# A transformer block on one core: queries times cosines read from the projection's bank, S5's output from inputs ahead of that from states, and operands of the last norms copied to PSUM

## The chip, the core and the metric

The kernel runs on one core of a Trainium2 chip. The metric is the device time of one execution in microseconds (us), the median of the runs. Five engines run side by side, each through its own queue of instructions in a fixed order: TensorE (PE, with its weight loads PEld), VectorE (DVE), ScalarE (ACT), GpSimd (POOL) and SyncE (SP), which here only issues DMA transfers. An instruction that waits holds up all that stand behind it on its engine.

## What is computed

The reference is one block on a sequence of 1024 tokens of width 1024, all in float32, cut here to its skeleton:

```python
proj = x @ w_in + b_in
q, k, v, u, xr, gate = split(proj)            # 512, 128, 128, 256, 256, 256 columns
q, k = apply_rope(q), apply_rope(k)           # t*cos + swapped(t)*sin, per head of 64
y_attn = sliding_window_attention(q, k, v, sinks)
y_s5   = s5_mixer(u, ...)                     # complex diagonal scan, then y = C h + D u, gelu, gated
y_lru  = rg_lru_mixer(xr, gate, ...)          # convolution, gates, real scan
mix = group_rmsnorm((y_attn, y_s5, y_lru), g)
x = layer_norm(ALPHA * x + mix @ w_out + b_out, ln1_g, ln1_b)
f = (silu(conv(x @ w_gate)) * (x @ w_up)) @ w_down        # inner width 2816
x = layer_norm(ALPHA * x + f, ln2_g, ln2_b)
```

## The kernel before

Most float32 products are made as three products of a high and a low part (`mm3`, lines 144 to 146); ACT writes the high part and DVE subtracts it to get the low one (`split`, lines 119 and 120). So each weight (`whi`, `wlo`) passes through ACT and then DVE before PE can use it. All large SBUF tiles come from one pool of 47 slots of 128x1024 floats, all PSUM tiles from one pool of eight banks of 128x512 floats.

The work stands in three stages. `mixers` makes the projections of x tile by tile (`project`, each tile of 128 columns in two halves of 512 tokens, a half being 24 products into a bank `pin`, which ACT copies out with the bias, line 527), and beside them S5, the RG-LRU and the attention, whose steps are Python generators that a table (AGENDA) starts after given projections. A scheduler then puts the instructions of each engine in an order by its own estimate of times, so that the order on each queue is that of the order listings below and not quite that of the source.

- Rotation of a query tile (`turn`): SP copies the halves of each head, swapped, to `rsw` (line 639). DVE multiplies the tile by the cosines, both operands in SBUF (line 645, 128x1024), POOL multiplies `rsw` by the sines (646), DVE adds (647), then ACT and DVE split the sum in `qh` and `ql`, and three DMAs stack those (670 to 672). There are four query tiles.
- S5's output: for each of two halves h, eight products of inputs U with `Tz` (line 443) alternate with eight of states H with `CA` (444) in two banks; each pair fills one 128-column piece of a bank. ACT applies gelu (446), SP writes Y to DRAM in eight pieces (449) and reads it back in another layout (452), loads the gate's weight (457), and PE makes the gate product (469). The states come from DVE and POOL (lines 228 to 233), are moved by SP (431), and U has been there long before.
- `ffn` makes gate and up products and at its end the down product by a seven-product scheme (D_ORDER = 1, 2, 6, 7, 5, 4, 3, each of 11 items, 77 in all). Each item loads two tiles (`d_load`), splits them (`d_parts`) and makes 12 products in four banks (`d_product`). `d_load(i + 9)` and `d_parts(i + 5 + ...)` say how many items ahead of product i the loads and the splits are issued. The last `LAST` items are made bank by bank, so that the four token blocks 0 to 3 end one after another; the last bank is made in two halves of 256 columns.
- The last norm: blocks 4 to 7 end with product 4 and are normed during product 3, blocks 0 to 2 after their banks end (`norm`), block 3 last of all (lines 1520 to 1525). `norm` takes mean and variance, ACT scales each half of 512 columns (1462), then DVE does the first half and POOL the second half, each a product with `ln2_g` (1463) and a sum with `ln2_b` (1464) on SBUF operands, and SP writes the block out.

Of the kernel before, what the change touches and what calls it, by code (L numbers as in the profile page):

```python
# [13 lines left out]
AF = mybir.ActivationFunctionType  # L14
ALU = mybir.AluOpType
MULT, ADD, SUB, MAX, MIN = ALU.mult, ALU.add, ALU.subtract, ALU.max, ALU.min
# [30 lines left out]
L = 1024  # L47
# [9 lines left out]
NC5 = L // T5  # L57
# [20 lines left out]
class Trunk:  # L78
# [163 lines left out]
    def s5(self, ud):  # L242

        nc, I = self.nc, self.I
        v, po, S = nc.vector, nc.gpsimd, self.small
# [15 lines left out]
        x = S([128, NP], "s5x")  # L261
# [83 lines left out]
        Tz = []  # L345
# [88 lines left out]
        dy = self.dr.tile([NG, CH, T5, NC5], F32, name="dy")  # L434
        yg = []
        for h in range(2):
            Y = self.big([128, 8, NC5], f"s5Y{h}")
            pY = [self.ps([128, 4, NC5], f"s5pY{q}") for q in range(2)]
            for i in range(4):
                pr = h * 4 + i  # L440
                for q in range(2):
                    o = pY[q][:, i, :]
                    nc.tensor.matmul(o, Tz[q][:, pr, :], U[h][:, 2 * i + q, :], start=True, stop=False)
                    nc.tensor.matmul(o, CA[q][:, pr, :], H[h][:, q, i, :], start=False, stop=True)
            for q in range(2):
                nc.scalar.activation(Y.rearrange("p (r q) c -> p q r c", q=2)[:, q], pY[q], AF.Gelu_apprx_tanh)
            yield
            for i in range(T5):
                nc.sync.dma_start(out=dy[h * 8:h * 8 + 8, :, i, :].rearrange("g c t -> c g t"),
                                  in_=Y[i * CH:(i + 1) * CH])  # L450
            y = self.big([128, T5, NC5], f"s5y{h}")
            nc.sync.dma_start(out=y.rearrange("p j t -> p (j t)"),
                              in_=dy[h * 8:h * 8 + 8].rearrange("g c j t -> (g c) (j t)"))
            yg.append(y)
# [70 lines left out]
    def in_half(self, W, f, hf, t, func=AF.Identity):  # L525
        p = self.proj_half(W, self.X, hf, "pin")
        self.nc.scalar.activation(t[:, hf * 512:(hf + 1) * 512], p, func, bias=self.col("b_in", f))


# [111 lines left out]

    def rope1(self, t, sw):

        nc = self.nc
        nc.vector.tensor_tensor(out=t, in0=t, in1=self.cos, op=MULT)
        nc.gpsimd.tensor_tensor(out=sw, in0=sw, in1=self.sin, op=MULT)
        nc.vector.tensor_tensor(out=t, in0=t, in1=sw, op=ADD)

# [25 lines left out]

    def turn(self, t, nm):

        sw = self.rope0(t)
        yield
        self.rope1(t, sw)
        hl = self.halves(t, nm)  # L680
        yield
        (self.stack_k if nm == "k" else self.stack_q)(hl)
        yield
# [409 lines left out]
    D_ORDER = (1, 2, 6, 7, 5, 4, 3)  # L1093
    LAST = 6

# [134 lines left out]
    def mixers(self):  # L1230
# [89 lines left out]
        def project(j):  # L1320
# [8 lines left out]
            t = at[nm, i]  # L1329
            self.in_half(Ws[nm, i], fs[nm] + i, hf, t, AF.Gelu_apprx_tanh if nm == "gg" else AF.Identity)  # L1330
            if hf:
                del Ws[nm, i]
                done[nm, i] = at.pop((nm, i))
                if nm in ("xr", "gg"):
                    (xr if nm == "xr" else self.gg).append(done.pop((nm, i)))
# [4 lines left out]
        def turn(nm, i):  # L1340
            yield from self.turn(done.pop((nm, i)), nm)

# [77 lines left out]
    def ffn(self, out):  # L1420
# [27 lines left out]
        ps = {}  # L1448
        g2 = b2 = None
        stats = lambda tb, i, s: v.bn_stats(bn[tb][:, i], self.z[tb][:, s])  # L1450
        hs = slice(0, 512), slice(512, D)

        def norm(tb):
# [5 lines left out]
            o = self.big([128, D], "o")  # L1459
            for h, e in enumerate((v, nc.gpsimd)):  # L1460
                s = hs[h]
                nc.scalar.activation(z[:, s], z[:, s], AF.Identity, scale=r, bias=m)  # L1462
                e.tensor_tensor(out=z[:, s], in0=z[:, s], in1=g2[:, s], op=MULT)  # L1463
                e.tensor_tensor(out=o[:, s], in0=z[:, s], in1=b2[:, s], op=ADD)
                if tb == 2:
                    nc.sync.dma_start(out=out[0, tb * 128:(tb + 1) * 128, s], in_=o[:, s])
# [4 lines left out]
        for i in range(cut):  # L1471
# [4 lines left out]
            b = ps[{2: "X", 7: "Q", 4: "Q"}.get(p, "T")]  # L1476
            self.d_load(i + 9)
            self.d_parts(i + 5 + (max(0, i - cut + 12) // 3))
            self.d_product(i, b, range(4), f == 0, f == NP_ - 1)
# [8 lines left out]
            if f == NP_ - 1:  # L1488
                for c in range(4):
                    self.d_out(p, c, b)  # L1490
                    if p in (2, 5, 4):
# [6 lines left out]
                        else:  # L1498
                            stats(tb, p == 5, hs[p == 5])
            if p == 3 and 0 < f < 5:  # L1500
                with self.after(self.mm.ins):
                    norm(3 + f)
        T = ps["T"]
# [14 lines left out]
        mv, a, r = st[tb]  # L1518
        for s in hs:
            v.scalar_tensor_tensor(z[:, s], z[:, s], mv[:, 0:1], g2[:, s], SUB, MULT)  # L1520
        self.newton(r, a)
        o = self.big([128, D], "o")
        for s in hs:
            v.scalar_tensor_tensor(o[:, s], z[:, s], r, b2[:, s], MULT, ADD)
            nc.sync.dma_start(out=out[0, tb * 128:(tb + 1) * 128, s], in_=o[:, s])
# [75 lines left out]
```

## Time and profile before

| | us |
|---|---|
| median of 3 runs | 1019.26 |
| lowest and highest of them | 1018.61, 1205.99 |
| the profiled execution, its own time | 1018.53 |
| its span, first to last instruction | 1016.5 |
| PE busy in it | 965.5 |
| DVE, POOL, ACT busy | 769.8, 563.2, 490.2 |

The span is that of one execution, and its own time is 2.0 us longer for what lies around it. A PE that is busy is counted with modelled ends of its matmuls, so a busy share of 95% is not a claim that PE is at its best; what is lost to waits and to a lower granted clock is read from the rows of single stretches.

### The profile page before, as it was taken

How to read it: one execution, taken by the hardware profiler on the slowest of the kernel's cores; microseconds unless marked ns; L12 is line 12 of the kernel's file. 1: busy time of each engine (PE TensorE's matmuls, PEld its weight loads, DVE VectorE, ACT ScalarE, POOL GpSimd, SP SyncE). 2: the span in 40 equal slices, each digit the busy share in tenths (PEclk: the TensorE clock that was granted, in tenths of full speed). 3: DMA queues.
4: the chain of work that ended last, by engine and by line, in shares of the span. 5: the costliest groups of instructions: out<-in, count | busy, mean ns of one | idle time of the engine just before them, and what ended most of it. 6: DMA issues, size and time to landing. Idle time of an engine off the chain costs nothing.

```text
span 1016.5 us, 13355 instructions
## 1 busy us (share of the span) xinstructions
PE 965.5 (95%) x4512; PEld 792.9 (78%) x4512; DVE 769.8 (76%) x1262; ACT 490.2 (48%) x952; POOL 563.2 (55%) x409
## 2 busy tenths in 40 slices
PE   8998888999999998999999999999999999999993
PEld 6877757789888776778878778888887788888883
DVE  6899668798989787667776777665676699965388
ACT  5322366676744766435524534545547265444131
POOL 0465234669843784777886878653551799000053
PEclk9999899999999999999999999999999999999997
DMA  8422665443221201546556546312415798686213
GB/s 301 145 54 82 150 164 144 116 115 110 77 105 63 82 22 42 191 182 228 197 204 240 197 176 233 151 68 88 155 73 186 284 391 287 211 289 202 64 42 124
DMA packets 64740, 158.53 MB, mean 156 GB/s; under 512 B 9440, under 2 KB 14080, under 8 KB 64672
## 3 DMA queue, kind: packets, MB, share of 16 engines
q1 hardware_dynamic: 64672, 157.68, 45.3%
q8 instruction: 35, 0.57, 0.2%
q14 instruction: 33, 0.27, 0.1%
HBM read 104.90 MB, written 42.21 MB: 145 GB/s over the span
## 4 chain that ended last, share of the span: by engine, by line
PE 55%; DVE 17%; POOL 9%; DMA 8%; issue 6%; ACT 4%; SPq 1%; DVEq 0%; POOLq 0%; ACTq 0%
PE pg L144 7%; PE pg L146 7%; PE pg L145 7%; PE pdT L145 3%; DMA d<-in_ffn_w_down_dram 3%; PE pdT L146 3%; PE pdT L144 3%; PE po L144 2%; PE po L146 2%; PE po L145 2%; PE pdQ L145 2%; PE pdQ L146 2%; POOL dt L1128 2%; PE pdQ L144 2%; POOL d L1128 2%
## 5 line engine op out<-in xcount | busy, mean ns | idle before, releaser
L120 DVE TENSOR_TENSOR dpl<-draw,dph 128x1024 fp32r<-128x1024 f32 x77 | 121.3, 1614 | 30.1 <-ACT dph L119 28.3
L144 PE MATMUL pg<-xt,apart 128*128 128x512 f32 x352 | 137.3, 391 | 4.1 <-ACT foa L1006 1.4
L146 PE MATMUL pg<-xt,apart 128*128 128x512 f32 x352 | 136.3, 391 | 2.5 <-DVE apart L120 2.4
L145 PE MATMUL pg<-xt,apart 128*128 128x512 f32 x352 | 137.3, 390 | 1.1 <-DVE xt L932 1.1
L119 ACT ACTIVATE dph<-draw 128x1024 fp32r<-128x1024 f32 x77 | 80.0, 1058 | 86.4 <-DVE dpl L120 24.5
L120 DVE TENSOR_TENSOR apart<-s,apart 128x512 fp32r<-128x512 f32 x88 | 94.7, 1086 | 25.4 <-ACT apart L119 25.3
L144 PE MATMUL pg<-xb,apart 128*128 128x512 f32 x264 | 103.2, 391 | 1.4 <-ACT fob L1006 1.4
L145 PE MATMUL pg<-xb,apart 128*128 128x512 f32 x264 | 102.8, 389 | 0.0
L146 PE MATMUL pg<-xb,apart 128*128 128x512 f32 x264 | 102.7, 389 | 0.0
L119 ACT ACTIVATE apart<-s 128x512 fp32r<-128x512 f32 x88 | 53.9, 626 | 63.8 <-POOL s L941 62.4
L144 PEld LDWEIGHTS pg<-xt,apart 128*128 128x128 f32 x352 | 66.1, 188 | 20.3 <-ACT foa L1006 3.6
L146 PEld LDWEIGHTS pg<-xt,apart 128*128 128x128 f32 x352 | 66.1, 188 | 18.8 <-DVE apart L120 5.3
L1463 POOL TENSOR_TENSOR z<-z,ln_g 128x512 f32<-128x512 f32 x7 | 11.5, 1643 | 123.3 <-ACT z L1462 123.3
L145 PEld LDWEIGHTS pg<-xt,apart 128*128 128x128 f32 x352 | 66.1, 188 | 15.4 <-DVE xt L932 1.9
L120 DVE TENSOR_TENSOR apart<-raw,apart 128x512 fp32r<-128x512 f32 x66 | 72.9, 1106 | 5.4 <-ACT apart L119 5.4
L145 PE MATMUL pdT<-dpl,dph 128*128 128x512 f32 (+1 forms) x182 | 69.6, 383 | 1.7 <-DVE dpl L120 1.7
L146 PE MATMUL pdT<-dph,dpl 128*128 128x512 f32 (+1 forms) x182 | 69.4, 382 | 0.0
L144 PE MATMUL pdT<-dph 128*128 128x512 f32 (+1 forms) x182 | 66.5, 383 | 0.6 <-DVE z L1205 0.5
L144 PEld LDWEIGHTS pg<-xb,apart 128*128 128x128 f32 x264 | 49.6, 188 | 12.6 <-ACT fob L1006 2.2
L1062 POOL TENSOR_TENSOR fc<-fc,fob 128x512 f32<-128x512 f32 x11 | 18.7, 1702 | 71.2 <-DVE fob L1005 62.8
L1086 DVE SCALAR_TENSOR_TENSOR fc<-pg,pack,fc 128x511 f32<-128x511 f32 (+1 forms) x64 | 46.4, 742 | 15.1 <-ACT tail L1083 10.9
L146 PEld LDWEIGHTS pg<-xb,apart 128*128 128x128 f32 x264 | 49.6, 188 | 10.3
(483 smaller groups left out, 2628.9 us busy)
## 6 DMA issues: line engine op xcount, KB each, us to landing
draw<-h SPq DMA_DIRECT2D x77, 256.0 KB, 5.3
raw<-in_ffn_w_gate_dram SPq DMA_DIRECT2D x22, 512.0 KB, 5.0
raw<-in_ffn_w_up_dram SPq DMA_DIRECT2D x22, 512.0 KB, 4.1
h<-fc SPq DMA_DIRECT2D x22, 512.0 KB, 2.6
d<-in_ffn_w_down_dram SPq DMA_DIRECT2D x22, 512.0 KB, 6.7
draw<-d SPq DMA_DIRECT2D x44, 256.0 KB, 5.4
draw<-in_ffn_w_down_dram SPq DMA_DIRECT2D x33, 256.0 KB, 5.4
h<-hs SPq DMA_DIRECT2D x11, 512.0 KB, 3.6
```

The source lines that it names most:

```text
L119: self.hi = nc.scalar.activation(hi, src, AF.Copy)
L120: e.tensor_tensor(out=lo, in0=src, in1=hi.bitcast(F32), op=SUB)
L144: self.mm = nc.tensor.matmul(out, ah, bh, start=first, stop=False, skip_group_check=more)
L145: nc.tensor.matmul(out, ah, bl, start=False, stop=False, skip_group_check=more)
L146: nc.tensor.matmul(out, al, bh, start=False, stop=last, skip_group_check=more)
L1062: e.tensor_tensor(out=c[:, one], in0=c[:, one], in1=x, op=MULT)
L1086: v.scalar_tensor_tensor(c[:, o + d:o + 512], g[:, 0:512 - d], cw(k), c[:, o + d:o + 512], MULT, ADD)
L1128: sub = lambda o, a, b: po.tensor_tensor(out=o, in0=a, in1=b, op=SUB)
L1463: e.tensor_tensor(out=z[:, s], in0=z[:, s], in1=g2[:, s], op=MULT)
```

## The change

It has four parts. The queries: in `project`, right after ACT's copy of a half, DVE reads the same PSUM bank, adds the bias, multiplies by the cosines and writes `qc` (eight instructions of 128x512); the four multiplications of line 645 for queries go, and the sum with `rsw` is made on `qc`. S5: all 16 products with inputs are put ahead of all 16 with states, in four banks. The last norms: ACT copies `ln2_g` and `ln2_b` into four PSUM banks at the end of product 4, and DVE's norm instructions take them from there; `norm` does POOL's half first on ACT; blocks 4 to 7 start one item earlier. The down product: `LAST` is 7, and the loads and splits of the last items are issued further ahead.

```diff
+        PY = [[self.ps([128, 4, NC5], f"s5pY{q}") for q in range(2)] for _ in range(2)]
+        for h in range(2):
+            for q in range(2):
+                for i in range(4):
+                    nc.tensor.matmul(PY[h][q][:, i, :], Tz[q][:, h * 4 + i, :], U[h][:, 2 * i + q, :], start=i == 0,
+                                     stop=False)
         for h in range(2):
             Y = self.big([128, 8, NC5], f"s5Y{h}")
-            pY = [self.ps([128, 4, NC5], f"s5pY{q}") for q in range(2)]
-            for i in range(4):
-                pr = h * 4 + i
-                for q in range(2):
-                    o = pY[q][:, i, :]
-                    nc.tensor.matmul(o, Tz[q][:, pr, :], U[h][:, 2 * i + q, :], start=True, stop=False)
-                    nc.tensor.matmul(o, CA[q][:, pr, :], H[h][:, q, i, :], start=False, stop=True)
+            pY = PY[h]
+            for q in range(2):
+                for i in range(4):
+                    nc.tensor.matmul(pY[q][:, i, :], CA[q][:, h * 4 + i, :], H[h][:, q, i, :], start=False, stop=i == 3)
...
-    LAST = 6
+    LAST = 7
...
+            if nm == "q":
+                if hf == 0:
+                    at["c", i] = self.big([128, L], "qc")
+                s = slice(hf * 512, hf * 512 + 512)
+                nc.vector.scalar_tensor_tensor(at["c", i][:, s], p, self.col("b_in", fs[nm] + i), self.cos[:, s], ADD, MULT)
...
-            for h, e in enumerate((v, nc.gpsimd)):
+            for h, e, g, b in ((1, nc.gpsimd, g2[:, hs[1]], b2[:, hs[1]]), (0, v, gb[0], gb[2])):
...
-            self.d_load(i + 9)
-            self.d_parts(i + 5 + (max(0, i - cut + 12) // 3))
+            self.d_load(i + 9 + max(0, i - 53) // 2)
+            self.d_parts(i + 5 + max(0, i - 46) // 2)
...
-            if p == 3 and 0 < f < 5:
+            if p == 4 and f == NP_ - 1:
+
+                for t in (g2, b2):
+                    for s in hs:
+                        x = self.ps([128, 512], "pgb")
+                        nc.scalar.activation(x, t[:, s], AF.Copy)
+                        gb.append(x)
+            if p == 3:
                 with self.after(self.mm.ins):
-                    norm(3 + f)
+                    norm(4 + f)
```

On PE, where S5's output begins (s5U are inputs, s5T the matrices for them, s5Hs the states, s5CA those for the states), the queue before reads:

```order
L443 MATMUL s5pY_1223<-s5U_418,s5T_787 128x128
L443 MATMUL s5pY_1224<-s5U_418,s5T_789 128x128
L443 MATMUL s5pY_1254<-s5U_489,s5T_787 128x128
L443 MATMUL s5pY_1255<-s5U_489,s5T_789 128x128
L444 MATMUL s5pY_1223<-s5Hs,s5CA 128x128
L443 MATMUL s5pY_1223<-s5U_418,s5T_787 128x128
```

and with the change:

```order
L440 MATMUL s5pY_1222<-s5U_418,s5T_787 128x128 x4
L440 MATMUL s5pY_1223<-s5U_418,s5T_789 128x128 x4
L440 MATMUL s5pY_1224<-s5U_489,s5T_787 128x128 x4
L440 MATMUL s5pY_1225<-s5U_489,s5T_789 128x128 x4
L447 MATMUL s5pY_1222<-s5Hs,s5CA 128x128 x4
L447 MATMUL s5pY_1223<-s5Hs,s5CA 128x128 x4
L144 MATMUL pin<-xah,whi 128x512
L145 MATMUL pin<-xal,whi 128x512
L146 MATMUL pin<-xah,wlo 128x512
```

Four products with inputs stood ahead of the first one with states; now it is sixteen. The products that follow (pin) are the same ones as before.

On DVE, where the first query tile is rotated (lam and lg belong to the RG-LRU, ssa to a norm), the queue before reads:

```order
L598 SCALAR_TENSOR_TENSOR lam<-lam,lg 128x512
L645 TENSOR_TENSOR q<-q,cos 128x1024
L789 TENSOR_SCALAR ssa<-ssp 128x4
L598 SCALAR_TENSOR_TENSOR lam<-lam,lg 128x512
L599 SCALAR_TENSOR_TENSOR lg<-lg,lxc 128x512
L647 TENSOR_TENSOR q<-q,rsw 128x1024
```

and with the change:

```order
L796 TENSOR_SCALAR ssa<-ssp 128x4
L1342 SCALAR_TENSOR_TENSOR qc<-pin,pack,cos 128x512
L602 SCALAR_TENSOR_TENSOR lam<-lam,lg 128x512
L603 SCALAR_TENSOR_TENSOR lg<-lg,lxc 128x512
L653 TENSOR_TENSOR qc<-qc,rsw 128x1024
```

The multiplication of the first tile is gone from here (its two halves stand further ahead), and in its place stands the second half of the second tile, which reads the bank of a projection that has just ended.

On DVE, from the sum that takes in PE's last products (the second 256-column piece of block 3; z_7278 is block 1, z_7280 block 2, z_7282 block 3), the queue before reads:

```order
L1205 TENSOR_TENSOR z_7282<-pdT,z_7282 128x256
L1463 TENSOR_TENSOR z_7278<-z_7278,ln_g 128x512
L1450 BN_STATS st<-z_7282 128x6
L1464 TENSOR_TENSOR o<-z_7278,ln_b 128x512
L848 RECIPROCAL rs<-rs 128x1
L804 TENSOR_SCALAR rst<-rs,lna 128x1
L805 TENSOR_SCALAR rst<-rst 128x1
L806 TENSOR_SCALAR rs<-rs,rst 128x1
L1458 TENSOR_SCALAR lnm<-mv,rs 128x1
L843 BN_AGGR mv<-st 128x2
L845 TENSOR_SCALAR lna<-mv 128x1
L1520 SCALAR_TENSOR_TENSOR z_7282<-z_7282,mv,ln_g 128x512 x2
```

and with the change (there z_7288 is block 2, z_7290 block 3):

```order
L1212 TENSOR_TENSOR z_7290<-pdT,z_7290 128x256
L1465 BN_STATS st<-z_7290 128x6
L850 BN_AGGR mv<-st 128x2
L1478 TENSOR_TENSOR z_7288<-z_7288,pgb 128x512
L852 TENSOR_SCALAR lna<-mv 128x1
L1542 SCALAR_TENSOR_TENSOR z_7290<-z_7290,mv,pgb 128x512 x2
L1479 TENSOR_TENSOR o<-z_7288,pgb 128x512
L855 RECIPROCAL rs<-rs 128x1
L811 TENSOR_SCALAR rst<-rs,lna 128x1
L812 TENSOR_SCALAR rst<-rst 128x1
L813 TENSOR_SCALAR rs<-rs,rst 128x1
L1546 SCALAR_TENSOR_TENSOR o<-z_7290,rs,pgb 128x512
```

The norm of block 1 and the small chain of block 2 stood behind that sum; now they stand ahead of it, and only block 2's two large instructions are left behind it with block 3's own.

## Rows read from the trace of the kernel before

**Rows 1.** What PE waited for: us in total, times, longest us
```profile
PE s5pY L444 <- DMA s5Hs<-s5H: 4.7, 1, 4.7
PE s5pg L469 <- DMA gluw<-in_s_glu_w_dram: 4.1, 1, 4.1
...
PE po L145 <- DVE wlo L123: 2.2, 1, 2.2
...
PE pdT L145 <- DVE dpl L120: 1.7, 2, 1.3
...
PE py L750 <- DVE z L838: 1.3, 1, 1.3
```

**Rows 2.** Stretches: PE, PEld, DVE, ACT, POOL busy, granted clock, DMA share, GB/s
```profile
104.00:108.00 4.00, 4.00 (x20) 4.00 (x20) 3.97 (x8) 0.60 (x1) 2.46 (x2) 0.50 0.01 4
...
204.00:208.00 4.00, 4.00 (x15) 3.29 (x15) 4.00 (x13) 3.79 (x12) 0.00 (x0) 0.61 0.99 284
```

**Rows 3.** Timeline of PE at S5's output: start, us, instruction, idle before
```profile
97.47 1.05 PE L443 MATMUL s5pY<-s5U,s5T 128*128 128x128 f32 x8
103.19 0.77 PE L444 MATMUL s5pY<-s5Hs,s5CA 128*128 128x128 f32 x2 [4.67 <-DMA s5Hs<-s5H]
...
110.57 0.50 PE L146 MATMUL pin<-xah,wlo 128*128 128x512 f32 x1 [1.21 <-DVE wlo L120]
```

**Rows 4.** Timeline of SP's queue from S5's states to the gate's weight
```profile
111.58 1.10 SPq L431 DMA_DIRECT2D s5Hs<-s5H  x2
...
121.81 5.69 SPq L449 DMA_DIRECT2D dy<-s5Y  x8
...
129.70 0.43 SPq L457 DMA_DIRECT2D gluw<-in_s_glu_w_dram  x1
```

**Rows 5.** Groups by line: the query's multiplications on DVE
```profile
L645 DVE TENSOR_TENSOR q<-q,cos 128x1024 f32<-128x1024 f32 x4 | 11.4, 2857 | 0.0
```

**Rows 6.** Timeline of DVE, queries and what follows them
```profile
153.26 1.21 DVE L645 TENSOR_TENSOR q<-q,cos 128x1024 f32<-128x1024 f32 x1
...
195.29 3.32 DVE L645 TENSOR_TENSOR q<-q,cos 128x1024 f32<-128x1024 f32 x1
...
199.53 2.89 DVE L647 TENSOR_TENSOR q<-q,rsw 128x1024 f32<-128x1024 f32 x1
202.34 1.27 DVE L123 SCALAR_TENSOR_TENSOR wlo<-wraw,pack,whi 128x1024 fp32r<-128x1024 f32 x1
...
212.88 0.73 DVE L838 SCALAR_TENSOR_TENSOR z<-po,rs,z 128x512 f32<-128x512 f32 x1
```

**Rows 7.** Timeline of POOL in the same stretch
```profile
195.13 2.39 POOL L646 TENSOR_TENSOR rsw<-rsw,sin 128x1024 f32<-128x1024 f32 x1
...
199.44 1.89 POOL L728 TENSOR_TENSOR smx<-smx,dn 128x1024 f32<-128x1024 f32 x1 [1.87 <-DVE dn L724]
...
212.08 1.92 POOL L728 TENSOR_TENSOR smx<-smx,dn 128x1024 f32<-128x1024 f32 x1
```

**Rows 8.** Timeline of ACT: a projection's copy, and a read of a shared bank
```profile
155.32 0.67 ACT L527 ACTIVATE q<-pin,pack 128x512 f32<-128x512 f32 x1
...
213.98 0.38 ACT L756 ACTIVATE y<-py 128x256 f32<-128x256 f32 x1 [0.86 <-DVE mal L754]
```

**Rows 9.** Timeline of DVE at the end
```profile
1002.88 0.42 DVE L1205 TENSOR_TENSOR z<-pdT,z 128x256 f32<-128x256 f32 x1
...
1004.40 1.61 DVE L1464 TENSOR_TENSOR o<-z,ln_b 128x512 f32<-128x512 f32 x1
...
1007.33 1.41 DVE L1520 SCALAR_TENSOR_TENSOR z<-z,mv,ln_g 128x512 f32<-128x512 f32 x2
...
1009.37 1.63 DVE L1464 TENSOR_TENSOR o<-z,ln_b 128x512 f32<-128x512 f32 x1
...
1011.66 1.67 DVE L1524 SCALAR_TENSOR_TENSOR o<-z,rs,ln_b 128x512 f32<-128x512 f32 x2
```

**Rows 10.** Timeline of PE at the end: its last wait for a split, its last product
```profile
992.49 0.50 PE L145 MATMUL pdT<-dpl,dph 128*128 128x512 f32 x1 [1.33 <-DVE dpl L120]
...
1002.57 0.28 PE L146 MATMUL pdT<-dph,dpl 128*128 128x256 f32 x1
```

More of the change, by code (lines that the diff above doesn't have):

```diff
@@ L527, in in_half @@
         self.nc.scalar.activation(t[:, hf * 512:(hf + 1) * 512], p, func, bias=self.col("b_in", f))
+        return p
     def lru_setup(self):
@@ L640, in rope0, with rope1 @@
         return sw
-    def rope1(self, t, sw):
+    def rope1(self, t, tc, sw):
         nc = self.nc
-        nc.vector.tensor_tensor(out=t, in0=t, in1=self.cos, op=MULT)
+        if tc is None:
+            tc = t
+            nc.vector.tensor_tensor(out=t, in0=t, in1=self.cos, op=MULT)
         nc.gpsimd.tensor_tensor(out=sw, in0=sw, in1=self.sin, op=MULT)
-        nc.vector.tensor_tensor(out=t, in0=t, in1=sw, op=ADD)
+        nc.vector.tensor_tensor(out=tc, in0=tc, in1=sw, op=ADD)
+        return tc
     def halves(self, t, nm):
@@ L673, in stack_q, with turn @@
         self.q += [hl[0], b]
-    def turn(self, t, nm):
+    def turn(self, t, tc, nm):
         sw = self.rope0(t)
         yield
-        self.rope1(t, sw)
+        t = self.rope1(t, tc, sw)
         hl = self.halves(t, nm)
@@ L1329, in project @@
             t = at[nm, i]
-            self.in_half(Ws[nm, i], fs[nm] + i, hf, t, AF.Gelu_apprx_tanh if nm == "gg" else AF.Identity)
+            p = self.in_half(Ws[nm, i], fs[nm] + i, hf, t, AF.Gelu_apprx_tanh if nm == "gg" else AF.Identity)
+            if nm == "q":
[3 more added lines that the diff above has]
+                nc.vector.scalar_tensor_tensor(at["c", i][:, s], p, self.col("b_in", fs[nm] + i), self.cos[:, s], ADD, MULT)
             if hf:
@@ L1333, in project @@
                 done[nm, i] = at.pop((nm, i))
+                if nm == "q":
+                    done["c", i] = at.pop(("c", i))
                 if nm in ("xr", "gg"):
@@ L1340, in turn @@
         def turn(nm, i):
-            yield from self.turn(done.pop((nm, i)), nm)
+            yield from self.turn(done.pop((nm, i)), done.pop(("c", i)) if nm == "q" else None, nm)
         def values():
@@ L1449, in ffn @@
         g2 = b2 = None
+        gb = []
         stats = lambda tb, i, s: v.bn_stats(bn[tb][:, i], self.z[tb][:, s])
@@ L1459, in norm @@
             o = self.big([128, D], "o")
-            for h, e in enumerate((v, nc.gpsimd)):
+            for h, e, g, b in ((1, nc.gpsimd, g2[:, hs[1]], b2[:, hs[1]]), (0, v, gb[0], gb[2])):
                 s = hs[h]
                 nc.scalar.activation(z[:, s], z[:, s], AF.Identity, scale=r, bias=m)
-                e.tensor_tensor(out=z[:, s], in0=z[:, s], in1=g2[:, s], op=MULT)
-                e.tensor_tensor(out=o[:, s], in0=z[:, s], in1=b2[:, s], op=ADD)
+                e.tensor_tensor(out=z[:, s], in0=z[:, s], in1=g, op=MULT)
+                e.tensor_tensor(out=o[:, s], in0=z[:, s], in1=b, op=ADD)
                 if tb == 2:
@@ L1518, in ffn @@
         mv, a, r = st[tb]
-        for s in hs:
-            v.scalar_tensor_tensor(z[:, s], z[:, s], mv[:, 0:1], g2[:, s], SUB, MULT)
+        for s, g in zip(hs, gb):
+            v.scalar_tensor_tensor(z[:, s], z[:, s], mv[:, 0:1], g, SUB, MULT)
         self.newton(r, a)
         o = self.big([128, D], "o")
-        for s in hs:
-            v.scalar_tensor_tensor(o[:, s], z[:, s], r, b2[:, s], MULT, ADD)
+        for s, b in zip(hs, gb[2:]):
+            v.scalar_tensor_tensor(o[:, s], z[:, s], r, b, MULT, ADD)
             nc.sync.dma_start(out=out[0, tb * 128:(tb + 1) * 128, s], in_=o[:, s])
```

## The prediction

> **What bounds the kernel now.** I read the table of times first: PE is busy 965.5 us of a span of 1016.5, so a change pays only where PE waits, where its clock is low, or behind its last product. Then the list of PE's waits [rows 1]: the long ones lie in the first 260 us, where S5, the queries and the attention feed PE, and one small one at the end. The change touches five of them. Then the stretches with a low granted clock [rows 2]: 0.50 from 104 to 108 us, after PE had stood 4.67 us, and 0.61 from 204 to 208, after it had stood 2.2; the level there is 1.2 GHz for part of the time or all of it. Last the end: PE's last product starts at 1002.57 [rows 10], and DVE is busy from 1002.88 to 1013.33 with what is left of the norms [rows 9]; the span ends 3.2 us after that, when the last block is written. So 14 us of the span lie behind PE.
>
> **S5's output.** Before, 8 records (four products of two records each) took 1.05 us, 0.13 each, and then PE stood until the states landed at 103.19 [rows 3]. Now 32 records stand there; the 24 further ones are 3.1 us of work inside the wait of 4.67, which leaves about 1.5. Behind the states, sixteen records then take 2.1 us at 0.13 each, or twice that at the lower clock, so PE is through at 105.3 to 107.4. But the third product behind them needs the low part of the next weight, for which PE stood until 110.57 [rows 3], on DVE, which had been busy with the second half of the states and does nothing for PE's new order. So all that the first half gains goes into that wait. The second half saves its share too (12 records, some 1.5 us), and what PE does then ends in the wait for the gate's weight, 4.1 us [rows 1]. That weight is issued by SP at 129.70 behind both halves of Y; SP's run begins at 111.58, when POOL's part of the states is done, and is held by its own issuing from there (the second eight writes alone 5.69 us) [rows 4]. None of that begins earlier. I take 0. Bounds: -4.1, if the gate's wait went with it, and +1, if the longer wait ahead of 110.57 costs clock on what follows and the second Y is late for SP at 121.81.
>
> **The queries.** Four multiplications go, 11.4 us of DVE, the first of them 1.21, so the other three 3.4 each [rows 5, 6]. The reason is in the rows: the one at 195.29 and POOL's multiplication at 195.13 (2.39 us) overlap, and it takes 3.32 [rows 6, 7]; so does the sum at 199.53, beside POOL at 199.44. An instruction of DVE with one operand in PSUM does not suffer: at 212.88 one of 128x512 takes 0.73 while POOL is busy from 212.08 to 214.00 [rows 6, 7]. Eight such cost 8 x 0.73 = 5.8 us, at times when DVE mostly stands.
>
> What it is worth is read at PE's wait for wlo of line 123 (2.2 us) [rows 1]. Before: multiplication 195.29 to 198.6, three small ones, sum 199.53 to 202.42, wlo 202.34 to 203.61. Now the sum can start when POOL has the sines, at 197.5; it takes 1.2 alone, or is pushed behind POOL's next multiplication by 1.9; wlo ends 1.3 later, at 200.0 to 201.9. PE waited 2.2 us for it, so it was ready at 201.4, and nearly the whole 2.2 goes. Against it stands a loss at the first tile. In the order listing its sum now stands behind the second tile's second half, which has to wait for ACT's copy, 155.32 to 155.99; before, the multiplication had started at 153.26 [rows 6, 8]. What hangs on it (ACT's split, then the next weight's) is 2.2 us later; most of this falls into two later waits of PE, and I carry 0.7 of it to here. Net -1.4, bounds +0.7 and -2.2. With the wait the low clock goes: 4 us at 0.61 are 1.56 us lost [rows 2]; I take -1.3, bounds 0 and -1.6. The wait of 1.3 us for z [rows 1], behind the fourth tile's multiplication, I count half, -0.6, bounds 0 and -1.3. Sum -3.3, with bounds +0.7 and -5.1.
>
> The new wait itself: ACT and DVE both only read the bank, and yet one waits for the other. Rows show the same pair before: ACT's y waits 0.86 us for DVE's mal, both reads of py [rows 8]. The Trainium skill says why, in "PSUM — Partial Sum Buffer", section "PSUM bank collisions raise a hardware error": accesses of two engines to one bank in the same partitions have to be kept apart, reads too. If that did not hold, the first tile would not be held up, and by this the sum would be 0.7 lower; the trace agrees with the page.
>
> **The end.** The splits further ahead fill a time in which DVE stood, and take three of them out of the norms of blocks 4 to 7. PE's wait of 1.33 at 992.49 goes with the slow product behind it: -1.5. The seventh item made bank by bank adds three products cut in two, which at 0.28 us for a cut one, overlapping [rows 10], is next to nothing. The short wait between the two halves of the last bank stays, since DVE must still read the first half ahead of the second.
>
> Behind the last product, DVE had 10.45 us: its sum 0.42, block 1's and block 2's product and sum (0.7 and 1.61, 0.7 and 1.63), block 3's two pairs 1.41 and 1.67, which makes 8.1, so 2.3 for small ones [rows 9]. The products' 0.7 is half of the pair of 1.41, in which POOL was idle. With the change, the listing has block 1 ahead of that sum. Left are 0.42, block 2's two at 0.7 (their operands are in PSUM, so POOL costs them nothing), block 3's two pairs at 1.41, and block 3's own small ones, 1.4 of the 2.3: 6.0 in all, so -4.4. What is late next: ACT's scaling of block 2, which now does POOL's half first and so gives DVE its half one instruction later; by my count it is ready as DVE comes to it. POOL's two for block 2 start as much earlier and end before block 3. ACT's four copies to PSUM fall between product 4 and the norms; ACT had nothing to do there. The end together is -5.9; bounds -3 (the stretch behind the last product keeps half its length to the chain over ACT) and -7.
>
> **Sum.** -3.3 - 5.9 = -9.2 against the profiled execution's 1018.53, which gives 1009.3. The median of the runs was 0.7 above that execution, so 1010.0. The likeliest case's own range is 1006 to 1013.
>
> **Rivals.**
> 1. Only the end pays. For it: DVE is busy nearly all of 200 to 208 [rows 2], and eight instructions more stand in its queue, each with a wait for ACT; against it: the wait for wlo has its cause in the two rows that change. Then the queries bring +0.7 and the end -5.9: 1019.3 - 5.2 = 1014.1.
> 2. S5 pays after all, as SP's queue moves up with PE's earlier Y: -4.1 more, 1005.9. Against it: what starts SP's run at 111.58 is POOL's part of the states [rows 4].
> 3. The end pays half, -3, with the queries as forecast: 1013. For it: ACT's turn for block 2 stands between.
> 4. DVE's queue is held. Each of the eight new instructions waits for ACT, and lam, lg and the attention's maxima wait behind it. At the first tile the hold is 2.7 us (153.26 to 155.99) [rows 6, 8]. If every one cost PE 1.5 us in a late weight, 12 us: 1019.3 - 5.9 + 12 = 1025, slower than before. It decides from 0.75 us of PE's time for each, where it eats up the end's gain. Against it: the other halves end when ACT has little ahead of them, and PE's next wait takes up what one hold costs.
> 5. The change doesn't do what it says: the operands in PSUM are no faster beside POOL. The row at 212.88 speaks against that; then 1018.
>
> **How the numbers follow.** My forecast 0.50, rival 1 0.24, rival 2 0.07, rival 3 0.12, rival 4 0.05, rival 5 0.02. The range goes from 1004 to 1016: it takes in rivals 1 and 3 and most of 2. A measurement of this kernel tells about 2% from no change, 20 us here, and hardly any case reaches that: faster by over 2% 0.03, within 2% 0.95, slower by over 2% 0.02.
>
> **What would show it.** Right: PE's wait for the states shrinks to 1.5 to 2 us, and the waits for wlo and for the gate's weight behind it grow by what was won; no low clock at 204; the sum of the third query tile ends by 201; DVE's last instruction 6 us behind PE's last product, and DVE's norms at 0.7 beside a busy POOL. Wrong: SP issues the gate's weight over 1 us earlier than 129.70; a wait of over 1 us that is new between 160 and 260; DVE's last part still over 8 us.

## The result, and the profile after

| | before | after |
|---|---|---|
| median of the runs, us | 1019.22 | 1007.69 |
| runs | 4, of them 1018.61, 1019.18, 1019.26 | 4, from 1006.64 to 1008.84 |
| the profiled execution, its span | 1018.53, 1016.5 | 1008.84, 1007.1 |

After is 0.9889 of before, 95% interval 0.987 to 0.9909: about 1% faster, short of the 2% at which this document speaks of a difference. The forecast was 1010.0, within 1004 to 1016. The profiled executions differ by 9.7 us, the medians by 11.5. One run each of before and of three kernels below (1206 to 5505 us) stands far above all others; it counts in the medians, which would be at most 0.6 lower without it, and not in the ratios.

What PE waited for, of the changed kernel (the columns are those of [rows 1]; the lines of the source have moved, L123 is still w_out's split):

```profile
PE pin L146 <- DVE wlo L120: 5.9, 3, 4.0
PE s5pg L472 <- DMA gluw<-in_s_glu_w_dram: 3.3, 1, 3.3
...
PE po L145 <- DVE wlo L123: 2.2, 2, 2.0
...
PE s5pY L447 <- DMA s5Hs<-s5H: 1.8, 1, 1.8
...
PE pdT L145 <- DVE dpl L120: 0.5, 1, 0.5
```

The wait for the states has shrunk from 4.7 to 1.8, and the one for wlo of the projections has grown to 5.9 in all. In the kernel before that one was:

```profile
PE pin L146 <- DVE wlo L120: 1.6, 2, 1.2
```

The waits for z ahead of py (1.3) and for dpl at the end (1.3) are gone. The wait for wlo of line 123, on which a term of the forecast rested, is 2.0 in this trace where it was 2.2. The same waits in PE's timeline, of the changed kernel:

```profile
102.92 2.02 PE L447 MATMUL s5pY<-s5Hs,s5CA 128*128 128x128 f32 x16 [1.80 <-DMA s5Hs<-s5H]
...
109.38 0.50 PE L146 MATMUL pin<-xah,wlo 128*128 128x512 f32 x1 [3.96 <-DVE wlo L120]
...
134.04 8.80 PE L472 MATMUL s5pg<-s5y,gluw 128*128 128x512 f32 x16 [3.32 <-DMA gluw<-in_s_glu_w_dram]
...
162.80 0.50 PE L146 MATMUL pin<-xah,wlo 128*128 128x512 f32 x1 [1.57 <-DVE wlo L120]
...
203.30 0.50 PE L145 MATMUL po<-wlo,msh 128*128 128x512 f32 x1 [2.01 <-DVE wlo L123]
```

Against [rows 3], what the states gain is waited for at 109.38, and the wait at 162.80 is new. The stretches of [rows 2] with one beside the first, of the changed kernel:

```profile
104.00:108.00 4.00, 1.41 (x11) 0.98 (x9) 3.97 (x5) 1.20 (x2) 3.63 (x2) 1.00 0.00 0
108.00:112.00 4.00, 2.62 (x9) 2.12 (x10) 3.93 (x4) 0.00 (x0) 2.28 (x2) 0.83 0.77 222
...
204.00:208.00 4.00, 3.90 (x26) 3.18 (x25) 4.00 (x13) 2.79 (x9) 0.00 (x0) 1.00 1.02 313
```

The granted clock at 104 is 1.00 (2.4 GHz), and the fall has moved to the stretch behind the longer wait, 0.83. At 204 it is 1.00 where it was 0.61. SP's queue, of the changed kernel, as [rows 4]:

```profile
110.39 1.10 SPq L431 DMA_DIRECT2D s5Hs<-s5H  x2
...
120.78 5.54 SPq L452 DMA_DIRECT2D dy<-s5Y  x8
...
128.54 0.43 SPq L460 DMA_DIRECT2D gluw<-in_s_glu_w_dram  x1
```

It starts 1.2 us earlier than before, and everything in it with it. The queries on DVE, of the changed kernel, as [rows 6]:

```profile
154.53 0.75 DVE L1342 SCALAR_TENSOR_TENSOR qc<-pin,pack,cos 128x512 f32<-128x512 f32 x1 [1.78 <-ACT q L530]
...
192.94 2.96 DVE L630 TENSOR_TENSOR gg<-lxc,gg 128x512 f32<-128x512 f32 x2
...
199.19 1.23 DVE L653 TENSOR_TENSOR qc<-qc,rsw 128x1024 f32<-128x1024 f32 x1
200.34 2.91 DVE L123 SCALAR_TENSOR_TENSOR wlo<-wraw,pack,whi 128x1024 fp32r<-128x1024 f32 x1
```

and POOL beside them, of the changed kernel, as [rows 7]:

```profile
193.16 2.19 POOL L735 TENSOR_TENSOR smx<-smx,dn 128x1024 f32<-128x1024 f32 x1 [0.34 <-DVE dn L731]
195.31 2.86 POOL L652 TENSOR_TENSOR rsw<-rsw,sin 128x1024 f32<-128x1024 f32 x1
...
199.34 2.83 POOL L735 TENSOR_TENSOR smx<-smx,dn 128x1024 f32<-128x1024 f32 x1 [0.22 <-PE ptp L109]
```

The third tile's sum ends at 200.42, where before it ended at 202.42. But the split behind it takes 2.91 instead of 1.27 and ends at 203.25, only 0.36 earlier than before: POOL's multiplication starts at 199.34 behind the sum's start, and the split at 200.34 behind POOL's. The sum itself starts at 199.19, only 0.34 earlier than before. Ahead of it the two RG-LRU multiplications by gg now take 2.96 together, beside POOL's at 193.16 and 195.31; in the kernel before they were:

```profile
192.09 0.66 DVE L626 TENSOR_TENSOR gg<-lxc,gg 128x512 f32<-128x512 f32 x1
192.76 0.65 DVE L626 TENSOR_TENSOR gg<-lxc,gg 128x512 f32<-128x512 f32 x1
```

The costliest groups of the parts that changed (busy us, mean ns of one, idle before), of the changed kernel:

```profile
L1478 POOL TENSOR_TENSOR z<-z,ln_g 128x512 f32<-128x512 f32 x7 | 9.0, 1290 | 120.2 <-ACT z L1477 120.2
L1479 POOL TENSOR_TENSOR o<-z,ln_b 128x512 f32<-128x512 f32 x7 | 9.0, 1288 | 0.3
...
L1342 DVE SCALAR_TENSOR_TENSOR qc<-pin,pack,cos 128x512 f32<-128x512 f32 x8 | 5.9, 744 | 6.3 <-ACT q L530 6.3
...
L1479 DVE TENSOR_TENSOR o<-z,pgb 128x512 f32<-128x512 f32 x7 | 4.8, 680 | 0.1
L1478 DVE TENSOR_TENSOR z<-z,pgb 128x512 f32<-128x512 f32 x7 | 4.7, 668 | 0.4 <-ACT z L1477 0.3
```

and the same four lines of the norms in the kernel before:

```profile
L1464 POOL TENSOR_TENSOR o<-z,ln_b 128x512 f32<-128x512 f32 x7 | 11.6, 1664 | 0.3
L1463 POOL TENSOR_TENSOR z<-z,ln_g 128x512 f32<-128x512 f32 x7 | 11.5, 1643 | 123.3 <-ACT z L1462 123.3
...
L1464 DVE TENSOR_TENSOR o<-z,ln_b 128x512 f32<-128x512 f32 x7 | 9.3, 1340 | 0.0
...
L1463 DVE TENSOR_TENSOR z<-z,ln_g 128x512 f32<-128x512 f32 x7 | 7.8, 1117 | 0.1
```

With an operand in PSUM, DVE's norm instructions take 0.67 to 0.68 each in the mean, beside a busy POOL too; before, the means were 1.12 and 1.34. POOL gains as well: 1.29 for one, where it had 1.64 and 1.66. DVE behind the last product, of the changed kernel, as [rows 9]:

```profile
998.11 0.42 DVE L1212 TENSOR_TENSOR z<-pdT,z 128x256 f32<-128x256 f32 x1 [1.01 <-PE pdT L146]
...
999.18 0.63 DVE L1478 TENSOR_TENSOR z<-z,pgb 128x512 f32<-128x512 f32 x1
...
999.79 1.40 DVE L1542 SCALAR_TENSOR_TENSOR z<-z,mv,pgb 128x512 f32<-128x512 f32 x2
1001.10 0.68 DVE L1479 TENSOR_TENSOR o<-z,pgb 128x512 f32<-128x512 f32 x1
...
1002.63 1.41 DVE L1546 SCALAR_TENSOR_TENSOR o<-z,rs,pgb 128x512 f32<-128x512 f32 x2
```

From 998.11 to 1004.04 are 5.93 us, where there were 10.45.

### The profile page after: what moved, and what is told of

It is laid out like the page before. It is cut to its first block, busy times and chain, and to the rows that moved or that the text cites. A ratio compares the mean times of both kernels' runs of the same rounds, so it can differ in the third digit from the quotient of the medians.

```text
span 1007.1 us, 13367 instructions
## 1 busy us (share of the span) xinstructions
PE 963.8 (96%) x4515; PEld 790.3 (78%) x4515; DVE 757.1 (75%) x1266; ACT 492.8 (49%) x956; POOL 558.3 (55%) x409
## 4 chain that ended last, share of the span: by engine, by line
PE 60%; DVE 12%; POOL 9%; DMA 7%; issue 6%; ACT 5%; SPq 1%; DVEq 0%; ACTq 0%; POOLq 0%
PE pg L144 9%; PE pg L146 9%; PE pg L145 9%; PE pdT L145 4%; PE pdT L146 4%; PE pdT L144 4%; DMA d<-in_ffn_w_down_dram 2%; PE po L144 2%; PE pdQ L145 2%; PE pdQ L144 2%; PE pdQ L146 2%; PE po L146 2%; PE po L145 2%; DMA qb<-qh 1%; PE pdX L145 1%
## 5 line engine op out<-in xcount | busy, mean ns | idle before, releaser
L120 DVE TENSOR_TENSOR dpl<-draw,dph 128x1024 fp32r<-128x1024 f32 x77 | 118.9, 1582 | 34.8 <-ACT dph L119 34.0
L1478 POOL TENSOR_TENSOR z<-z,ln_g 128x512 f32<-128x512 f32 x7 | 9.0, 1290 | 120.2 <-ACT z L1477 120.2
```

The source lines that it names most:

```text
L120: e.tensor_tensor(out=lo, in0=src, in1=hi.bitcast(F32), op=SUB)
L1478: e.tensor_tensor(out=z[:, s], in0=z[:, s], in1=g, op=MULT)
```

## The experiments

Runs of one kernel lie up to 8.5 us apart here, so beside the median each row has four stretches of its one trace, which start and end with the same instructions in every kernel. **A** goes from the first product with states (near 103 us) to the gate's first product (134); **C** from the product that waits for w_out's low part (203) to the transposes that wait for z (336); **P** from the product that waits for dpl near 807 to the start of PE's last product; **T** from there to the end of DVE's last instruction. A holds what S5 does, C the last part of what the queries do, P and T the end.

| kernel | median | ratio to before, interval | A | C | P | T |
|---|---|---|---|---|---|---|
| before, first trace | 1019.22 | | 32.51 | 135.32 | 192.15 | 10.76 |
| before, second trace | 1017.77 (1 run) | | 31.34 | 135.37 | 192.11 | 10.76 |
| changed, first trace | 1007.69 | 0.9889, 0.987 to 0.9909 | 31.12 | 132.59 | 190.58 | 6.25 |
| changed, second trace | 1007.09 | 0.9891, 0.9871 to 0.9911 | 30.28 | 132.65 | 190.55 | 6.25 |
| changed without S5's order | 1008.49 | 0.993, 0.991 to 0.9949 | 31.08 | 132.90 | 190.58 | 6.25 |
| changed without the queries | 1009.76 | 0.994, 0.9918 to 0.9961 | 30.65 | 134.91 | 190.55 | 6.25 |
| changed without the end | 1016.77 | 1.0006, 0.9987 to 1.0024 | 31.37 | 132.66 | 192.12 | 10.76 |
| before with S5's order | 1017.69 | 1.001, 0.9989 to 1.0031 | 31.19 | 134.38 | 192.19 | 10.77 |
| changed, old leads | 1011.17 | 0.9941, 0.9922 to 0.9959 | 30.99 | 132.63 | 190.55 | 9.04 |
| changed, norms from SBUF | 1014.01 | 0.9979, 0.9962 to 0.9995 | 30.79 | 132.67 | 196.25 | 6.87 |
| before with the new leads | 1015.49 | 0.999, 0.9977 to 1.0003 | 31.30 | 135.31 | 195.81 | 6.04 |

The median of the kernel before was 1017.46 beside the four kernels without S5's order, without the queries, without the end and with S5's order alone; 1016.70 beside the second trace of before and the other three kernels; and 1018.74, on another chip, beside the second trace of the changed kernel and those of the last experiment. The ratios are those on record and differ by up to 0.002, 2 us, from the quotients of these medians.

The medians do not add up. The changed kernel is 11.5 and 11.7 us under the kernel before that ran beside it; without S5's order it is 9.0 under, without the queries 7.7 and without the end 0.7. The three losses sum to some 17. What a part is worth is therefore read from the stretches.

### S5's order, taken out and put in alone

Its 16 products with inputs alternate with those with states again (no_s5); and only_s5 is the kernel before with the new order alone:

```diff
-                    nc.tensor.matmul(PY[h][q][:, i, :], Tz[q][:, h * 4 + i, :], U[h][:, 2 * i + q, :], start=i == 0,
-                                     stop=False)
...
+                    nc.tensor.matmul(o, Tz[q][:, pr, :], U[h][:, 2 * i + q, :], start=True, stop=False)
+                    nc.tensor.matmul(o, CA[q][:, pr, :], H[h][:, q, i, :], start=False, stop=True)
```

> The changed kernel with S5's output in its old order (products with inputs and with states alternating, two banks); all else as changed. Theory A, S5's order itself is worth nothing, and the 1.2 us by which DMA issues started earlier in the changed kernel's trace come from which of DVE and POOL got to its operands first near 95 us (POOL's product 1.64 us and DVE's 1.77 in the one trace, 2.24 and 0.68 in the other): then the time stays at the changed kernel's 1007.7, within 0.6, and either of the two cases near 95 us may show up here as well. Theory B, S5's order is worth the 1.7 us that the gate products start earlier: then 1009.4. In both, PE's wait for the states is back at 3.5 to 4.7 us.

> The kernel before with S5's new order alone. Theory A (worth nothing by itself): 1019.2, within 0.6. Theory B (1.7 us by an earlier gate's weight): 1017.5. The rival in which all of the gate's wait goes: 1015.1. In both, PE's wait for the states shrinks to 1.5 to 2 us, and what is won is waited for at the low part of the next weight.

Theory A holds by the stretches. Stretch A is 31.08 to 31.34 with the old order (the first trace of before apart) and 30.28 to 31.37 with the new one; the means, 31.24 and 30.91, are 0.3 us apart. The kernel before with S5's order alone gives a ratio of 1.001, which leaves no room for 4.1 us and little for 1.7. Against it stands the ratio of the changed kernel without S5's order, 0.993, about 4 us above the changed kernel's and outside its interval. Its one trace shows no place for them (a span of 1007.8, beside 1007.1 and 1006.4 of the changed kernel), but why its runs differ was not settled.

### The kernel before again: what happened near 95 us

No edit.

> The kernel before, unchanged, for a second trace of it. Theory A: the stretch from PE's wait for dpl near 808 us to its wait for z is 190.0 and the stretch from there to DVE's last instruction 12.9 in every run of it, so what differs between its runs lies ahead of 808 us: in which of DVE and POOL goes first near 95 us (PE's wait for the gate's weight then ends near 134.5 and not at 135.7), and in the low granted clock at single places. Rival: the end itself differs from run to run.

Its P and T are those of the first trace to 0.04 us: the end does not differ between the two. SP issues the gate's weight at 129.08 here, and at 129.70 in the first trace, though the states land 0.4 later. The timeline of POOL and DVE at S5's states, first trace of the kernel before:

```profile
95.47 1.64 POOL L231 TENSOR_TENSOR s5H<-s5Er,s5t 128x508 f32<-128x508 f32 x1 [5.69 <-DVE s5t L421]
95.89 1.77 DVE L229 TENSOR_TENSOR s5ht<-s5Ei,s5t 128x508 f32<-128x508 f32 x1
```

and the second trace of the same kernel:

```profile
96.03 2.24 POOL L231 TENSOR_TENSOR s5H<-s5Er,s5t 128x508 f32<-128x508 f32 x1 [5.69 <-DVE s5t L421]
96.45 0.68 DVE L229 TENSOR_TENSOR s5ht<-s5Ei,s5t 128x508 f32<-128x508 f32 x1
```

In the one POOL went first and DVE waited, in the other DVE, for the same instructions of the same program. All other traces here, of either order of S5, have 2.23 to 2.25 and 0.68. From the start of POOL's product to SP's second load of the states there are 16.11 us in the first trace, 15.03 in the second and 15.02 in the changed kernel's. So 1.1 of the 1.2 us by which SP's run started earlier in the changed kernel's trace are this, and not the change.

### The queries, taken out

```diff
-                nc.vector.scalar_tensor_tensor(at["c", i][:, s], p, self.col("b_in", fs[nm] + i), self.cos[:, s], ADD, MULT)
```

> The changed kernel with the queries' old multiplication from SBUF (128x1024, four times on DVE) and no read of the projection's bank by DVE. The prediction's term (-3.3) gives 1011.0. Its rival (the queries bring +0.7) gives 1007.0. By the traces, the first 260 us gained about 2.6 in all, of which 1.1 belong to what happened near 95 us, so 1.5 is left for the queries: 1009.2. The low clock at 204 to 208 us should be back, with PE's wait for the low part of w_out at 203 us about 2 us as in both traces.

Measured 1009.76, 2.1 over the changed kernel's first median; the old stretch C is back, 134.91. Over the traces of the table, C is 134.38 to 135.37 (mean 135.06 of five) with the old multiplications and 132.59 to 132.90 (mean 132.68 of six) with the new ones: 2.4 us. PE's wait of 1.29 for z ahead of py is in each of the five and in none of the six, and the low clock at 204 comes and goes with it, as this window of the kernel without the queries shows:

```profile
204.00:208.00 4.00, 4.00 (x24) 3.81 (x23) 4.00 (x12) 3.42 (x12) 0.29 (x2) 0.64 0.96 262
```

0.57 to 0.66 in the five, 1.00 in the six. From the gate's products to 203 us, their own duration apart (7.1 to 8.8 by the clock), PE takes 59.3 to 61.5 with the old multiplications (mean 60.4) and 60.0 to 61.1 with the new ones (mean 60.4): nothing is gained there, within the 1 us or so by which single traces scatter. The wait at 203 itself is 2.25 to 2.62 in the five and 0.77 to 2.02 in the six, but other waits ahead of it, that at 162.80 above all, have taken up what it lost.

The same traces show what DVE's time at 192 to 203 us went into. With the old multiplications the pair by gg takes 1.31 or 1.32, the sum 2.88 or 2.89 and the split 1.27, in each of the five; with the new ones 2.95 or 2.96, 1.23 and 2.91 or 2.92, in each of the six. The multiplication went and the sum became shorter, and the pair and the split became longer in their place, each beside a multiplication of POOL. That POOL holds them is read from these rows; no edit moved POOL's multiplications away.

### The first tile alone

The first query tile is multiplied from SBUF as before, the other three from the bank (q0_old).

```diff
-            if nm == "q":
+            if nm == "q" and i:
```

> The changed kernel with the first query tile multiplied from SBUF as before and the other three from the projection's bank. It tells what the hold of DVE at the first tile costs (its sum stands behind the second tile's read of the bank, which waits 1.78 us for ACT). Prediction's account: PE's new wait of 1.57 us at 162.80 goes, and 0.7 us of it is left in the total, 1007.0. Theory now: the wait for the next weight's high part near 170 grows from 0.95 to about 1.7, as in the kernels with the old multiplications, and nothing is left, 0 within 0.5. Rival: all of it is left, -1.6.

Median 1008.77, ratio 0.9894 (0.9874 to 0.9914), against 1007.09 and 0.9891 of the changed kernel on the same chip. No gain, as the theory said; but the interval is wider than the 0.7 in question, and no trace of it could be used to read the waits from, so this term stays open.

### The end, taken apart

no_end puts the whole end back, end_last6 the leads and LAST alone, end_sbuf the operands alone; only_leads has the new leads and LAST in the kernel before.

```diff
-    LAST = 7
+    LAST = 6
...
-            self.d_load(i + 9 + max(0, i - 53) // 2)
-            self.d_parts(i + 5 + max(0, i - 46) // 2)
+            self.d_load(i + 9)
+            self.d_parts(i + 5 + (max(0, i - cut + 12) // 3))
```

is the edit of end_last6, together with the norms of blocks 4 to 7 put back one item, and

```diff
-                        x = self.ps([128, 512], "pgb")
-                        nc.scalar.activation(x, t[:, s], AF.Copy)
-                        gb.append(x)
+                        gb.append(t[:, s])
```

that of end_sbuf.

> The changed kernel with the old end: LAST 6, loads and splits as before, norms with SBUF operands and DVE's half first. By the prediction's term (-5.9) 1013.6; by the traces (PE -1.6, DVE behind it -4.5) 1013.8; by the rival that the end pays half, 1010.7. DVE's last instruction stands 10 to 10.5 us behind PE's last product again.

> The changed kernel with LAST 6, the loads, splits and norms of blocks 4 to 7 as far ahead as before, but the norms' operands still in PSUM and POOL's half first. Theory A (each part is worth what the traces show in it): PE's stretch from its wait for dpl at 807 us to its wait for z at the end is back from 188.1 to 190.0, and nothing else: 1.9 more than the changed kernel, 1009.6, with runs within 2 us of each other. Theory B (the old, shorter lead is also what spreads the runs of the kernels with the old end over 8 us, 1012 to 1020, where the changed kernel has 1006.6 to 1008.8): a median of 1012 to 1014 and runs spread over 6 us or more.

> The changed kernel with the norms' operands read from SBUF (no copies to PSUM); LAST 7, the leads and POOL's half first stay. Theory A: only the stretch from PE's wait for z at the end to DVE's last instruction changes, 8.74 us now and 12.9 with the old end. If the operands' place makes the whole of it, 12.9 and 1011.9; if only DVE's two instructions of block 2 (1.63 to 0.68) and block 3's pairs beside POOL (1.67 to 1.41) pay, and the three splits that left the stretch do the rest, 10 to 11 and 1009 to 1010. Rival: the place is worth nothing, and it stays at 8.7.

> The kernel before with LAST 7 and the loads, splits and norms of blocks 4 to 7 further ahead, alone: no operands in PSUM, DVE's half first, queries and S5 as before. Theory A: 1.9 us less than before. Theory B (the leads also take away the spread): the runs lie within 2 to 3 us of each other, and the median is 3 us or more under the kernel before's beyond these 1.9.

P and T together are 202.9 before and 196.8 after: 6.1 us. Without the end all 6.1 are back, with 202.88. Its median is 9.1 over the changed kernel's first, though, and by its ratio of 1.0006 the queries would bring nearly nothing, where its own stretch C has their 2.4; that was not settled.

The parts do not add up. Operands in PSUM with the old leads bring 3.3 (P 190.55, T 9.04). New leads with operands in SBUF bring 1.1 (only_leads), or lose 0.2 where POOL's half is scaled first (end_sbuf). Both together bring 6.1. Theory A of end_last6 fell: P stayed at 190.55, and it was T that grew. Theory A of end_sbuf fell the other way: T changed by 0.6 and P grew by 5.7. The kernel before with the new leads gained 1.1 of the 1.9 expected, and its runs still spread over 4.8. Theory B of end_last6 fell too: the spread that it expected of the old leads is there (1007.72 to 1013.66), but the kernel with the new leads and SBUF has the same (1011.87 to 1017.78). PE at the end of the kernel with norms from SBUF:

```profile
996.94 0.58 PE L144 MATMUL pdT<-dph 128*128 128x256 f32 x1 [4.72 <-DVE z L1212]
```

and DVE there:

```profile
995.34 1.15 DVE L1478 TENSOR_TENSOR z<-z,ln_g 128x512 f32<-128x512 f32 x1
...
996.48 0.41 DVE L1212 TENSOR_TENSOR z<-pdT,z 128x256 f32<-128x256 f32 x1
996.81 1.36 DVE L1479 TENSOR_TENSOR o<-z,ln_b 128x512 f32<-128x512 f32 x1
```

The norms (1.15 and 1.36, beside a busy POOL) stand ahead of the last sums, DVE comes to those later, and PE's last half bank waits 4.72 us for a sum (0.52 with operands in PSUM). So the leads move DVE's work from behind PE to before its end, and only with the faster instructions does it fit there. The reverse, PSUM with the old leads, on DVE behind the last product (995.95):

```profile
997.07 0.67 DVE L1478 TENSOR_TENSOR z<-z,pgb 128x512 f32<-128x512 f32 x1
...
1000.92 0.69 DVE L1478 TENSOR_TENSOR z<-z,pgb 128x512 f32<-128x512 f32 x1 [0.60 <-ACT z L1477]
```

Block 1's norm (997.07) still stands behind PE, and block 2's, at 1000.92, behind it; that is the 2.8 us of T.

### The changed kernel again, and its gate weight loaded earlier

The changed kernel without an edit:

> The changed kernel, unchanged, for a second trace of it and its time on the chip of the other runs. Its stretches should be as in the first trace: 188.1 us from PE's wait for dpl near 807 us to its wait for z, 8.74 from there to DVE's last instruction, 132.6 to 132.9 from the products with w_out near 203 us to the transposes near 336 (135.0 to 135.4 in the kernel before). If the runs of all these kernels spread alike, its runs lie over 4 us or more and not over 2, with a median of 1007 to 1010.

Median 1007.09, runs from 1006.09 to 1011.83, and every stretch as expected. The other kernel issues the load of the gate's weight before the writes of Y; glu_q0 adds the edit of the first tile.

```diff
+        nc.sync.dma_start(out=self.gw, in_=I["s5_glu_w"][0].rearrange("(k p) o -> p k o", p=128))
...
         dy = self.dr.tile([NG, CH, T5, NC5], F32, name="dy")
...
-        nc.sync.dma_start(out=self.gw, in_=I["s5_glu_w"][0].rearrange("(k p) o -> p k o", p=128))
```

> The changed kernel with the load of the gate's weight issued behind the loads of the states and ahead of the writes of Y, and not behind the last of them. PE's wait of 3.3 us for it at 134 us is then a wait for the second half of Y, read back into SBUF at about 132.8 (issued at 128.15, 4.6 us to landing). Theory: the gate's products start 1.2 us earlier, and the kernel is 1.2 us faster. Rival: the later waits of PE for the weights of the next tiles (1.57, 0.95 and 0.39 between 162 and 172 us) take it up, and the time is the same within 0.4.

> Both edits of the two kernels ahead together. If both gains pass through, 1.2 + 0.7 under the changed kernel; if later waits take them up, the same time within 0.5.

Measured 1012.69 (ratio 0.9947, 0.9928 to 0.9966), 5.6 slower than the changed kernel, and 1010.44 with both edits: neither theory. PE of the kernel with the early load:

```profile
132.16 3.60 PE L472 MATMUL s5pg<-s5y,gluw 128*128 128x512 f32 x8
...
140.60 3.60 PE L472 MATMUL s5pg<-s5y,gluw 128*128 128x512 f32 x8
...
166.17 0.76 PE L144 MATMUL pin<-xah,whi 128*128 128x512 f32 x1 [4.23 <-ACT whi L119]
```

The wait of 3.3 us is gone, and the gate's products start 1.9 earlier. But the scheduler, which orders by its own estimates, has cut them in two, so that the second eight end at 144.20, where the changed kernel had all sixteen done at 142.84, and given the engines another order behind them; a wait of 4.23 for whi came in place of 1.57 and 0.95. No kernel here has a lower median than the changed one.

## Why the prediction was right, and where it was not

**The total.** -9.2 was forecast; the spans of two traces each of before (1016.5, 1015.3) and after (1007.1, 1006.4) differ by 9.2, the medians by 11.5. The terms measured in the stretches are -0.3 for S5, -2.4 for the queries and -6.1 for the end, -8.8. The 2.7 us by which the medians go further are not placed; the runs' spread is larger. That the sum comes this near is in part luck: within the queries a term that failed and one that paid twice its forecast offset each other by half.

**S5: right, by its own reason.** The wait for the states is 1.8 (1.5 to 2 was forecast), and the wait for wlo took the rest: 3.96 instead of 1.21. SP issued the gate's weight 1.2 us earlier, which the prediction had named as a sign of being wrong. The second trace of before and the two S5 kernels show that it was not S5. The wait for the gate's weight, which was to grow, is 3.3 where it was 4.1; in all traces of the table it lies between 1.15 and 4.06, so it tells nothing of S5.

**The queries: -3.3 forecast, -2.4 measured; the step that failed is the wait for wlo of line 123.** The prediction let the sum be held by POOL's next multiplication at the worst and gave the split behind it 1.3 us. What happened has two halves. The sum was to start at 197.5, when POOL has the sines. POOL had them at 198.17, and the sum started at 199.19, since DVE came to it late: the pair by gg ahead of it took 2.96 instead of 1.31. Then the sum passed first, POOL's multiplication second, and the split, which reads two SBUF tensors itself, took 2.91. So the low part came only 0.36 earlier; the term of -1.4 is 0, as far as the stretch up to 203 us shows. The Trainium skill states the rule that the step applied to one instruction only, in "SBUF — State Buffer", section "Who interferes with whom": a DVE instruction with two SBUF inputs contends with a GpSimd instruction that reads SBUF, and the one that comes first holds the shared ports for its whole length. The trace agrees, with 1.23, 2.83 and 2.91 in turn. Which one comes first is not told by the starts in the rows: near 95 us POOL's row starts 0.42 ahead of DVE's in both traces of before, and yet DVE's is the one lengthened in the first (1.77 instead of 0.68) and POOL's in the second (2.24 instead of 1.64).

The other two steps were mis-sized or had the wrong reason. The wait for z ahead of py went wholly, -1.29 and not half of it. The low clock at 204 went, as forecast, though the wait just before did not: PE still stood 2.01, and the clock stayed at 1.00. In the eleven traces PE stood 2.25 to 2.62 there where the clock fell (0.57 to 0.66), and 0.77 to 2.02 where it did not. Whether the shorter wait alone keeps the clock up was not tried. The hold at the first tile is there (1.78 us for ACT, and PE's new wait of 1.57 at 162.80, over the 1 us that the prediction had set as a sign of being wrong), and is taken up by 203 us, as far as the stretch to there shows.

**The end: right in both sizes, with a partly wrong reason.** PE was to gain 1.5 and gained 1.57; DVE's part behind PE was to go from 10.45 to 6.0 and went to 5.93. But PE's wait for dpl at 992.49 was put down to the leads. With the old leads and operands in PSUM it is gone too, and with the new leads and operands in SBUF a longer wait (3.80 or 4.72, for z) comes in its place. So either edit takes that wait away, but only the operands shorten PE's stretch (P 190.55 with them alone, 195.81 with the leads alone). The leads alone pay almost nothing, 1.1, which the prediction did not see.

**The rivals.** Only the end pays (1014.1): no, C shows 2.4. S5 pays by SP's queue (1005.9): A shows 0.3 and the ratio of S5's order alone nothing; the ratio without S5's order, 0.993, stays unexplained. The end pays half: that is what the operands alone would have done, 3.3. DVE's queue held eight times: three of the eight reads waited, 6.3 us in all, and only the wait at 162.80 behind the first tile was followed up in PE. That DVE's read of the bank comes behind ACT's is what the Trainium skill makes one expect, in "PSUM — Partial Sum Buffer", section "PSUM bank collisions raise a hardware error"; the trace agrees, with DVE's wait of 1.78 for ACT. The operands in PSUM no faster: 0.67 beside 1.29 on POOL.

## What to carry to other kernels

Where DVE and POOL worked side by side here, one PSUM operand per DVE instruction made the instructions of both shorter (1.12 and 1.34 to 0.67 and 0.68, and 1.64 and 1.66 to 1.29); free banks at the end of a kernel are a place for broadcast vectors. Work that is moved ahead of PE's end pays only if it is short enough to fit there: measure the two edits together and apart. And when an instruction escapes a contended port, ask which instructions ahead of it and behind it now meet the holder.

## What the runs showed of the hardware that was not expected

Which of DVE and POOL goes first at a contended place changes between executions of one program: 1.64 and 1.77 in one trace of before, 2.24 and 0.68 in the next, and in the first of them SP's queue from the states on starts 1.1 us later. Beside that, the last fifth of the kernel repeats to 0.08 us between executions (P 190.53 to 190.58 in all kernels with the norms' operands in PSUM, 192.11 to 192.19 in those with the whole old end), while the runs of one kernel lie up to 8.5 us apart; in these traces, what differs between executions lies ahead of that part.
